# Delta rule's norms: sums of squares with the tokens as moving columns on column tiles, one root and reciprocal for four tiles, factors spread from row tiles

## The chip, the cores and the metric

One core of a Trainium2 chip runs the whole program in one launch. Its engines work side by side, each through its own instruction list in order: TensorE (PE, matmuls; PEld is its weight load), VectorE (DVE), ScalarE (ACT), GpSimd (POOL), and the queues that start DMAs (SP's above all). The metric is the device time of one execution in microseconds; the kernel before has a median of 2775.28 us over three runs (2774.92 to 2777.58).

## The reference, cut to what matters

The program is one block with a dilated attention and a gated delta rule, followed by two blocks of another kind, on 512 tokens of width 1024, in fp32. The change touches the norms of the first block's delta rule (8 heads of 64):

```python
def _l2norm(x):
    return x * lax.rsqrt(jnp.sum(x * x, axis=-1, keepdims=True) + EPS)

def _gated_deltanet(q, k, v, z, b_logit, a_logit, conv_w, a_log, dt_bias, norm_g):
    qkv = jax.nn.silu(_causal_conv(jnp.concatenate([q, k, v], axis=-1), conv_w))
    ...
    q = _l2norm(q.reshape(shp)) * HEAD_DIM ** -0.5
    k = _l2norm(k.reshape(shp))
    ...
    o = _chunk_gated_delta_rule(q, k, v, g, beta)
    o = _rmsnorm(o, norm_g) * jax.nn.silu(z.astype(jnp.float32).reshape(shp))
```

So each token has one factor per head for q, one for k, and later one for the output o.

## The kernel before

Activations lie feature by token: a tile is 128 partitions (features, two heads of 64) by 512 tokens, and the delta rule's q, k and v are four such tiles each (t = 0 to 3). A projection (`proj`, L133) is 24 matmuls of 512 columns into a PSUM tile of tag mm (3 buffers); its weights come by DMA, and ScalarE and VectorE split them into two fp32r parts (L103, L104). Everything else on PE writes PSUM tiles of tag mx (5 buffers).

`mixer1` (L581) writes its work in an order by hand: a list `d` of projections is worked off by `d.need` (up to a name) and `d.fill` (a number of microseconds' worth), and between them stand the steps of the delta rule. A scheduler then orders the instructions of every engine by priority, which follows the order written, and gives out the buffers; on the chip every engine goes through its list in that order, so a waiting instruction holds back what is behind it on its engine.

For tile t, L987 to L1000: `d.need("d{t}")` (three projections with convolution, `delta_in` L661), `delta_norm(t)` (L701), `delta_tok(t)` (L716: transposes of k and v), `delta_pairs(t)` (L732: products k by k and q by k, per head, times a decay), `q_decay(t)` (L759).

The norm itself: ScalarE squares q and k (L705). `head_rstd` (L680) sums each head's 64 features: a square's 128 x 128 piece is the stationary operand and two columns of ones (`bones`) move, so that the sums come out with tokens on partitions, 128 x 16 for q and k (L687). Root and reciprocal run on these (L467, L468). To bring the factors back to 512 columns, one column of them, repeated 64 times, is stationary and the identity moves (L696), 8 matmuls of 128 columns for q and as many for k. VectorE multiplies (L707).

At the end of `mixer1`, L1053 to L1060, `delta_out(t)` (L876) computes o for tile t (L886, L891), squares it (L894), multiplies by gain and gate (L897), and takes `head_rstd` for the one tile, then multiplies and splits into yd (L899, L900), which the last half of w_out's projection (`into_x`) reads.

Of the kernel before, what the change touches and what calls it, by code (L numbers as in the profile page):

```python
# [30 lines left out]
def cap(ap, off, dims):  # L31
    return bass.AP(ap.tensor, ap.offset + off, [list(ap.ap[0])] + [list(d) for d in dims])
# [37 lines left out]
class Net:  # L70
# [510 lines left out]
    def mixer1(self, extra, norm):  # L581
        nc, A, V = self.nc, self.A, self.V[0]
        v = nc.vector
# [93 lines left out]
                                       op0=ALU.mult, op1=ALU.add)  # L677
            nc.scalar.activation(out=dst, in_=dst, func=AF.Silu)

        def head_rstd(sqs):  # L680

            ps = self.mx()
            n = len(sqs)
            for j, sq in enumerate(sqs):
                for t in range(4):
                    c = 8 * j + 2 * t
# [5 lines left out]
            for j in range(n):  # L692
                ps = self.mx()
                for t in range(4):
                    for e in range(2):
                        nc.tensor.matmul(out=ps[64 * e:64 * e + 64, t * P:(t + 1) * P], lhsT=cap(c, 8 * j + 2 * t + e, [[0, 64]]),  # L696
                                         rhs=self.ident, start=True, stop=True)
                out.append(ps)
            return out

        def delta_norm(t):  # L701
            sqs = []
            for j in range(2):
                sqs.append(self.t2("dsq"))
                nc.scalar.activation(out=sqs[j], in_=qkv[j, t], func=AF.Square)  # L705
            for j, r in enumerate(head_rstd(sqs)):
                v.scalar_tensor_tensor(out=qkv[j, t], in0=qkv[j, t], scalar=0.125 if j == 0 else 1.0, in1=r,  # L707
                                       op0=ALU.mult, op1=ALU.mult)

        kdec = self.t8("kdec")  # L710
# [48 lines left out]
        def q_decay(t):  # L759
            eg = self.t2("eg")  # L760
            for e in range(2):
                nc.sync.dma_start(out=eg[64 * e:64 * e + 64],
                                  in_=bass.AP(es.tensor, es.offset + (2 * t + e) * T, [[0, 64], [1, T]]))
            v.tensor_tensor(out=q_all[:, t], in0=q_all[:, t], in1=eg, op=ALU.mult)
            nc.scalar.copy(out=st["egl"][:, t], in_=cap(eg, 63, [[64, 8]]))
# [107 lines left out]
            zs[t] = zs["all"][:, t]  # L873
            nc.scalar.activation(out=zs[t], in_=ps, func=AF.Silu)

        def delta_out(t):  # L876
            if t == 0:
                y[1] = [self.t8("yd", F32R) for _ in range(2)]
            ps = self.mx()
            S = st["S"]  # L880
            hs = [(2 * t + e, slice(64 * e, 64 * e + 64)) for e in range(2)]

            for tt in range(4):
                sl = slice(tt * P, tt * P + P)
                for h, o in hs:
                    nc.tensor.matmul(out=ps[o, sl], lhsT=rv[h // 4][:, tt, h % 4, 0:64], rhs=qkm[h // 4][:, h % 4, sl],  # L886
                                     start=tt == 0, stop=False)
            for c in range(1, 8):
                sl = slice(64 * c, 64 * c + 64)
                for h, o in hs:  # L890
                    nc.tensor.matmul(out=ps[o, sl], lhsT=S[o, c, 64 * t:64 * t + 64], rhs=q_all[o, t, sl],  # L891
                                     start=False, stop=c == 7)
            sq = self.t2("osq")
            nc.scalar.activation(out=sq, in_=ps, func=AF.Square, scale=0.125)  # L894
            yield
            o = self.t2("od")
            v.scalar_tensor_tensor(out=o, in0=ps, scalar=dng, in1=zs[t], op0=ALU.mult, op1=ALU.mult)  # L897
            r = head_rstd([sq])[0]
            v.tensor_tensor(out=o, in0=o, in1=r, op=ALU.mult)  # L899
            self.split(y[1][0][:, t], y[1][1][:, t], o)  # L900


        va = self.t8("va")
# [83 lines left out]
        for t in range(4):  # L987
            d.need(f"d{t}")
            if t == 0:
                d.need("ba")  # L990
            delta_norm(t)
            delta_tok(t)
            delta_pairs(t)
            q_decay(t)
            if t == 0:
                self.stash()
                self.load_rows()
            if t == 2:
                clear()
            d.fill(4, "va")  # L1000
        steps = solve()
        next(steps)
        self.setup2()
# [50 lines left out]
        next(outs[0])  # L1054
        for t in range(4):
            if t < 3:
                next(outs[t + 1])
            d.fill(C / 2)
            for _ in outs[t]:
                pass  # L1060
# [571 lines left out]
```

## Time and profile before

| | |
|---|---|
| profiled execution, device time | 2775.28 us |
| its span, first to last instruction | 2773.5 us |
| PE busy | 2708.2 us, 98% |
| VectorE busy | 1716.4 us, 62% |
| ScalarE busy | 1169.8 us, 42% |
| mean granted clock of PE, share of full speed | 0.991 |

Times are microseconds from the span's start. A matmul's length in a row is that of its way through the array, and the next one starts before it ends; what a matmul costs PE is the time to the next start. An fp32 matmul is two records (passes), an fp32r one is one. "[1.39 <-ACT dsq L705]" says how long the engine was idle before, and what ended it.

### The profile page before, as it was taken

What the parts mean: (1) busy time and instruction counts of PE and PEld (TensorE: products, weight loads), DVE (VectorE), ACT (ScalarE), POOL (GpSimd) and SP (SyncE); (2) the same over time, 40 slices, a digit from 0 to 9 for tenths busy, and PEclk for the clock granted to TensorE, in tenths of its full rate; (3) what the DMA queues carried; (4) which work ended last, traced back from release to release, by engine and by line L of the source; (5) the groups of instructions that cost most, each with busy time, mean ns of one, the idle gap of its engine ahead of it and who ended that gap; (6) DMA issues with size and microseconds to landing.
All of it is one profiled execution on the core that took longest, in us unless ns stands there. A gap on an engine that the chain in (4) does not pass through costs nothing. (4 is left out here: it accounts for less than half of the span.)

```text
span 2773.5 us, 42593 instructions
## 1 busy us (share of the span) xinstructions
PE 2708.2 (98%) x17518; PEld 2201.5 (79%) x17518; DVE 1716.4 (62%) x2690; ACT 1169.8 (42%) x1792; POOL 41.7 (2%) x79
## 2 busy tenths in 40 slices
PE   8999899999999999999999999999999999999998
PEld 4786678888887887887888888887877878888887
DVE  4687656747378777757466563568787575533334
ACT  5644333323255545444343232466454453422223
POOL 0011000000000000100000000000000000000000
PEclk9999999999999999999999999999999999999999
DMA  7464534646332222332446463322223334333332
GB/s 244 129 183 122 150 121 152 213 155 218 88 106 70 63 81 69 111 99 79 133 132 229 143 230 91 102 77 63 76 69 103 92 84 136 91 93 98 99 98 77
DMA packets 471315, 330.66 MB, mean 119 GB/s; under 512 B 15447, under 2 KB 426223, under 8 KB 469584
## 3 DMA queue, kind: packets, MB, share of 16 engines
q1 hardware_dynamic: 468176, 320.51, 38.1%
q0 software_dynamic: 2944, 7.43, 0.9%
q8 instruction: 138, 2.26, 0.3%
q14 instruction: 57, 0.47, 0.1%
HBM read 312.55 MB, written 13.24 MB: 117 GB/s over the span
## 5 line engine op out<-in xcount | busy, mean ns | idle before, releaser
L103 ACT CAST whi<-raw 128x1024 fp32r<-128x1024 f32 (+2 forms) x451 | 439.0, 975 | 1057.0 <-PE mm L124 748.7
L123 PE MATMUL mm<-hh,whi 128*128 128x512 f32 (+1 forms) x2248 | 865.4, 388 | 10.6 <-ACT hh L495 9.0
L124 PE MATMUL mm<-hl,whi 128*128 128x512 f32 (+1 forms) x2248 | 867.3, 386 | 1.6 <-DVE hl L496 1.2
L125 PE MATMUL mm<-hh,wlo 128*128 128x512 f32 (+1 forms) x2248 | 866.4, 386 | 0.0
L104 DVE TENSOR_TENSOR wlo<-raw,whi 128x1024 fp32r<-128x1024 f32 (+2 forms) x451 | 507.4, 1127 | 355.3 <-ACT whi L103 333.5
L123 PEld LDWEIGHTS mm<-hh,whi 128*128 128x128 f32 x2248 | 421.6, 189 | 102.7 <-ACT hh L495 12.9
L124 PEld LDWEIGHTS mm<-hl,whi 128*128 128x128 f32 x2248 | 424.4, 189 | 89.6 <-DVE hl L496 4.3
L125 PEld LDWEIGHTS mm<-hh,wlo 128*128 128x128 f32 x2248 | 424.2, 189 | 88.0 <-issue 4.6
L124 PE MATMUL mm<-hid,whi 128*128 128x512 f32 (+1 forms) x564 | 212.5, 377 | 0.0
L123 PE MATMUL mm<-hid,whi 128*128 128x512 f32 (+1 forms) x564 | 212.3, 376 | 0.0
L125 PE MATMUL mm<-hid,wlo 128*128 128x512 f32 (+1 forms) x564 | 211.9, 376 | 0.0
L500 DVE SCALAR_TENSOR_TENSOR x<-mm,mod,x 128x512 f32<-128x512 f32 (+1 forms) x116 | 80.4, 694 | 176.8 <-PE mm L125 176.0
L315 DVE SCALAR_TENSOR_TENSOR acc<-araw,cs,acc 128x512 f32<-128x512 f32 x224 | 167.9, 750 | 21.3 <-DMA araw<-in_w_ada_dram 16.5
L550 DVE TENSOR_TENSOR sg<-mm,sg 128x512 f32<-128x512 f32 x66 | 45.6, 691 | 149.6 <-PE mm L125 147.8
L1180 DVE TENSOR_TENSOR R<-R,tot 128x512 f32<-128x512 f32 x192 | 126.6, 685 | 10.1 <-PE mx L1145 7.1
L202 PE MATMUL mm<-wlo,hh 128*128 128x256 f32 x448 | 129.3, 289 | 0.8 <-DVE wlo L104 0.8
L203 PE MATMUL mm<-whi,hl 128*128 128x256 f32 x448 | 129.8, 290 | 0.0
L201 PE MATMUL mm<-whi,hh 128*128 128x256 f32 x448 | 129.0, 288 | 0.0
L123 PEld LDWEIGHTS mm<-hid,whi 128*128 128x128 f32 x564 | 106.1, 188 | 20.3 <-issue 1.2
L125 PEld LDWEIGHTS mm<-hid,wlo 128*128 128x128 f32 x564 | 106.1, 188 | 19.2
L124 PEld LDWEIGHTS mm<-hid,whi 128*128 128x128 f32 x564 | 106.1, 188 | 19.2
L202 PEld LDWEIGHTS mm<-wlo,hh 128*128 128x128 f32 x448 | 87.5, 195 | 1.7 <-DVE wlo L104 1.2
(376 smaller groups left out, 3359.2 us busy)
## 6 DMA issues: line engine op xcount, KB each, us to landing
raw<-in_w_in_dram SPq DMA_DIRECT2D x164, 512.0 KB
araw<-in_w_ada_dram SPq DMA_DIRECT2D x48, 1024.0 KB
raw<-in_w_ffn_in_dram SPq DMA_DIRECT2D x88, 512.0 KB
araw<-in_w_ada_dram SPq DMA_DIRECT2D x64, 256.0 KB
raw<-in_w_ffn_out_dram SPq DMA_DIRECT2D x32, 512.0 KB
raw<-in_w_gate_dram SPq DMA_DIRECT2D x22, 512.0 KB
raw<-in_w_up_dram SPq DMA_DIRECT2D x22, 512.0 KB
raw<-in_w_ada_dram SPq DMA_DIRECT2D x16, 512.0 KB
```

The costliest lines, as they stand in the source:

```text
L103: self.nc.scalar.copy(out=hi, in_=src)
L104: self.nc.vector.tensor_tensor(out=lo, in0=src, in1=hi.bitcast(F32), op=ALU.subtract)
L123: m(out=ps, lhsT=w[0], rhs=a[0], start=first, stop=False)
L124: m(out=ps, lhsT=w[0], rhs=a[1], start=False, stop=False)
L125: return m(out=ps, lhsT=w[1], rhs=a[0], start=False, stop=last)
L201: m(out=o, lhsT=a[0][:, sl], rhs=hi[:, k % 4], start=k == 0, stop=False)
L202: m(out=o, lhsT=a[0][:, sl], rhs=lo[:, k % 4], start=False, stop=False)
L203: m(out=o, lhsT=a[1][:, sl], rhs=hi[:, k % 4], start=False, stop=k == KT - 1)
L315: nc.vector.scalar_tensor_tensor(out=acc, in0=raw, scalar=cs[:, k:k + 1], in1=acc, op0=ALU.mult, op1=ALU.add)
L500: self.nc.vector.scalar_tensor_tensor(out=self.x(f)[:, sl], in0=ps[:, sl], scalar=g[:, f:f + 1], in1=self.x(f)[:, sl], op0=ALU.mult, op1=A ...
L550: nc.vector.tensor_tensor(out=sg, in0=pu, in1=sg, op=ALU.mult)
L1180: v.tensor_tensor(out=o, in0=o, in1=half(1 - c), op=ALU.mult)
```

## The change

Sums: the ones are now stationary (32 columns of `bones`: 16 for the one head, 16 for the other) and the square moves, 512 tokens at once, into one of the four 32-partition column tiles of a PSUM tile (`head_sums`, L686 of the new kernel). Four tiles' sums (q and k of two t) share one PSUM tile; one root and one reciprocal of 128 x 512 serve all (`head_factors`, L692, L693). Spread: a column that picks one row of a 32-row tile, repeated 64 times, is stationary and the 32 x 512 factors move (`head_spread`, L702), two matmuls for each of the four, from row tile 32c into column half 64e. `delta_norm` works on two t at once; `delta_out` is a generator over two t, with roots on 64 x 512.

```diff
-        def head_rstd(sqs):
-            ps = self.mx()
...
-                    nc.tensor.matmul(out=ps[:, c:c + 2], lhsT=sq[:, t * P:(t + 1) * P], rhs=cap(bones, 0, [[64, 2]]),
-                                     start=True, stop=True)
-            c = self.sp.tile([P, 16], F32, name="hc", tag="hc", bufs=2)
-            self.rsqrt(c[:, :8 * n], ps[:, :8 * n])
...
+        pick = consts[:, 448:450]
+        for e in range(2):
+            v.tensor_tensor(out=pick[:, e:e + 1], in0=i64[:, 16 * e:16 * e + 1], in1=i64[:, 32 + 16 * e:33 + 16 * e], op=ALU.add)
+
+        def head_sums(sq, ps, c):
+            nc.tensor.matmul(out=ps[32 * c:32 * c + 32], lhsT=bones[:, 48:80], rhs=sq, start=True, stop=True,
+                             tile_position=(0, 32 * c))
+
+        def head_factors(ps, n):
+            r = self.t2("hr")
+            nc.scalar.activation(out=r[:32 * n], in_=ps[:32 * n], func=AF.Sqrt, bias=self.eps[:32 * n])
+            v.reciprocal(out=r[:32 * n], in_=r[:32 * n])
+            return r
+
+        def head_spread(r, cs):
             out = []
+            for c in cs:
+                out.append(self.mx())
+                for e in range(2):
+                    nc.tensor.matmul(out=out[-1][64 * e:64 * e + 64], lhsT=cap(pick[32 * c:32 * c + 32], e, [[0, 64]]),
+                                     rhs=r[32 * c:32 * c + 32], start=True, stop=True, tile_position=(32 * c, 64 * e))
             return out
...
-        for t in range(4):
-            d.need(f"d{t}")
...
-            delta_norm(t)
-            delta_tok(t)
-            delta_pairs(t)
-            q_decay(t)
...
-            d.fill(4, "va")
+        for t in (0, 2):
+            ps = self.mx()
+            for u in (t, t + 1):
+                d.need(f"d{u}")
...
+                delta_sums(u, ps)
+            r = head_factors(ps, 4)
+            d.fill(C, "va")
+            delta_norm((t, t + 1), r)
+            for u in (t, t + 1):
+                delta_tok(u)
+                delta_pairs(u)
+                q_decay(u)
...
+                d.fill(4, "va")
...
-        outs = [delta_out(t) for t in range(4)]
...
+        a, b = [delta_out((2 * i, 2 * i + 1)) for i in range(2)]
+        next(a)
+        next(a)
+        d.fill(C / 2)
+        next(a)
+        next(b)
+        d.fill(C / 2)
+        next(b)
+        for _ in a:
+            pass
+        d.fill(C / 2)
+        next(b)
+        d.fill(C)
+        for _ in b:
+            pass
```

The order of the instructions moves with it. On PE before, from the first tile's spread (L696) to its pair products (L748); L123 to L125 are a projection's matmuls, L720 the transposes:

```order
L696 MATMUL mx<-c_ident,hc 64x128 x16
L125 MATMUL mm<-hh,wlo 128x512
L123 MATMUL mm<-hh,whi 128x512
L124 MATMUL mm<-hl,whi 128x512
...
L720 MATMUL mx<-c_ident,k_all 128x128 x4
L720 MATMUL mx<-c_ident,vd 128x128 x4
L748 MATMUL mx<-k_all 128x128 x8
L748 MATMUL mx<-q_all,k_all 128x128 x8
```

Six projection matmuls stand between, and 44 behind, before the next tile's sums. Now, from the spread of tiles 0 and 1 (L702) through both blocks (L728 are the transposes, L756 the products, with the buffers' numbers):

```order
L702 MATMUL mx_713<-hr_701,consts_367 64x512 x2
L728 MATMUL mx_720<-c_ident_83,k_all_387 128x128 x4
L728 MATMUL mx_727<-c_ident_83,vd_495 128x128 x4
L756 MATMUL mx_743<-k_all_387 128x128
L756 MATMUL mx_744<-k_all_387 128x128
...
L756 MATMUL mx_753<-q_all_386,k_all_387 128x128
L756 MATMUL mx_754<-q_all_386,k_all_387 128x128
...
L728 MATMUL mx_802<-c_ident_83,k_all_387 128x128 x4
L728 MATMUL mx_809<-c_ident_83,vd_687 128x128 x4
L123 MATMUL mm_905<-hh_264,whi_900 128x512
L756 MATMUL mx_825<-k_all_387 128x128 x3
```

Both tiles' blocks now follow each other with one projection matmul between them, and none between spread and transposes.

On DVE now, behind the pair's reciprocal (L693), where L715 are the multiplications by the factors, L736 and L738 read the transposes, L760 and L763 the products, and L746 and L747 make the decay (gb):

```order
L693 RECIPROCAL hr_701<-hr_701 128x512
L104 TENSOR_TENSOR wlo_984<-raw_982,whi_983 128x1024
L746 TENSOR_TENSOR gb_733<-gb_733,rt_385 128x512
L715 SCALAR_TENSOR_TENSOR q_all_386<-q_all_386,mx_704 128x512
L715 SCALAR_TENSOR_TENSOR k_all_387<-k_all_387,mx_707 128x512
L715 SCALAR_TENSOR_TENSOR q_all_386<-q_all_386,mx_710 128x512
L747 SCALAR_TENSOR_TENSOR gb_733<-gb_733,consts_367 128x512
L715 SCALAR_TENSOR_TENSOR k_all_387<-k_all_387,mx_713 128x512
L736 TENSOR_TENSOR kdec_390<-mx_720,rt_385 128x4x128
L738 TENSOR_TENSOR rr_391<-mx_720,rt_385 128x4x2x64
L746 TENSOR_TENSOR gb_738<-gb_738,rt_385 128x512
L760 TENSOR_TENSOR nt_763<-mx_743,gb_733 128x512
```

The four multiplications of two tiles stand together, ahead of the first tile's kdec, rr and nt, where before each tile had its own two ahead of its own block.

## Rows read from the trace of the kernel before

**Rows 1.** the page's busy times, whole span

```profile
PE 2708.2 (98%) x17518; PEld 2201.5 (79%) x17518; DVE 1716.4 (62%) x2690; ACT 1169.8 (42%) x1792; POOL 41.7 (2%) x79
```

**Rows 2.** table by stretch: length, busy per engine (instructions), clock, DMA, GB/s

```profile
80.00:172.00 92.00, 86.04 (x634) 73.89 (x633) 69.87 (x107) 57.34 (x82) 11.22 (x18) 0.94 0.49 150
...
373.00:402.00 29.00, 28.05 (x324) 23.26 (x324) 14.29 (x26) 10.03 (x18) 0.00 (x0) 1.00 0.09 26
```

**Rows 3.** instructions of L687 and L696: ns min/median/max, first and last start, form

```profile
L687 PE MATMUL mx<-consts,dsq x64: 165/251/353, 80.8 to 158.9; 128*128 128x2 f32 x64
...
L696 PE MATMUL mx<-c_ident,hc x192: 272/273/476, 85.9 to 395.3; 128*64 128x128 f32 x192
```

**Rows 4.** timeline, first tile's norm: start, length, engine, instruction, [idle before]

```profile
80.81 1.02 PE L687 MATMUL mx<-consts,dsq 128*128 128x2 f32 x8
...
81.69 0.47 PE L123 MATMUL mm<-hh,whi 128*128 128x512 f32 x1
...
85.94 1.97 PE L696 MATMUL mx<-c_ident,hc 128*64 128x128 f32 x32
...
87.84 0.19 PEld L125 LDWEIGHTS mm<-hh,wlo 128*128 128x128 f32 x1 [0.17 <-issue]
```

**Rows 5.** PE's timeline around L395, column tiles of 32

```profile
20.96 1.05 PE L395 MATMUL mx<-raw,cz 128*32 128x512 f32 x4
21.94 1.16 PE L483 MATMUL mx<-c_ident,col 128*128 128x128 f32 x8
...
31.95 1.07 PE L395 MATMUL mx<-raw,cz 128*32 128x512 f32 x8
```

**Rows 6.** timeline of the pair products, two row halves

```profile
90.31 1.16 PE L748 MATMUL mx<-k_all 64*128 64x128 f32 x16
...
91.30 1.34 PE L748 MATMUL mx<-q_all,k_all 64*128 64x128 f32 x16
```

**Rows 7.** instructions of L454, L453 and L468: ns min/median/max

```profile
L454 DVE RECIPROCAL rstd<-rstd x24: 3343/3353/3354, 882.3 to 2286.7; 128x512 f32<-128x512 f32 x24
...
L453 ACT ACTIVATE rstd<-mx,eps x24: 677/688/691, 881.6 to 2285.9; 128x512 f32<-128x512 f32 x24
...
L468 DVE RECIPROCAL hc<-hc x8: 194/228/253, 83.8 to 393.7; 128x16 f32<-128x16 f32 x4, 128x8 f32<-128x8 f32 x4
```

**Rows 8.** PE's waits, 30 to 175 us: total, times, longest

```profile
PE mx L687 <- ACT dsq L705: 3.7, 2, 2.3
...
PE mm L123 <- ACT q_all L673: 1.6, 1, 1.6
...
PE mx L646 <- DVE gt L643: 0.7, 1, 0.7
```

**Rows 9.** timeline of the projections' matmuls, at either clock

```profile
95.29 0.63 PE L124 MATMUL mm<-hl,whi 128*128 128x512 f32 x1
...
95.71 0.63 PE L125 MATMUL mm<-hh,wlo 128*128 128x512 f32 x1
...
98.88 0.39 PE L125 MATMUL mm<-hh,wlo 128*128 128x512 f32 x1
...
99.11 0.39 PE L123 MATMUL mm<-hh,whi 128*128 128x512 f32 x1
```

**Rows 10.** DVE's timeline behind the second tile's spread

```profile
111.80 0.69 DVE L707 SCALAR_TENSOR_TENSOR q_all<-q_all,mx 128x512 f32<-128x512 f32 x1 [2.68 <-PE mx L696]
112.40 0.68 DVE L738 TENSOR_TENSOR gb<-gb,rt 128x512 f32<-128x512 f32 x1
```

**Rows 11.** timeline of delta_out, first tile's norm

```profile
377.29 1.05 PE L687 MATMUL mx<-consts,osq 128*128 128x2 f32 x8
...
378.20 0.47 PE L125 MATMUL mm<-ya,wlo 128*128 128x512 f32 x1
...
381.02 1.09 PE L696 MATMUL mx<-c_ident,hc 128*64 128x128 f32 x16 [0.95 <-DVE hc L468]
...
381.95 1.04 PE L886 MATMUL mx<-qkm,rr 128*64 128x128 f32 x16
```

More of the change, by code (lines that the diff above doesn't have):

```diff
@@ L678, in delta_in @@
             nc.scalar.activation(out=dst, in_=dst, func=AF.Silu)
-        def head_rstd(sqs):
-            ps = self.mx()
-            n = len(sqs)
-            for j, sq in enumerate(sqs):
-                for t in range(4):
-                    c = 8 * j + 2 * t
-                    nc.tensor.matmul(out=ps[:, c:c + 2], lhsT=sq[:, t * P:(t + 1) * P], rhs=cap(bones, 0, [[64, 2]]),
-                                     start=True, stop=True)
-            c = self.sp.tile([P, 16], F32, name="hc", tag="hc", bufs=2)
-            self.rsqrt(c[:, :8 * n], ps[:, :8 * n])
-            out = []
[L692 to L698, printed above, removed]
-            return out
@@ L705, in delta_norm @@
-                nc.scalar.activation(out=sqs[j], in_=qkv[j, t], func=AF.Square)
-            for j, r in enumerate(head_rstd(sqs)):
-                v.scalar_tensor_tensor(out=qkv[j, t], in0=qkv[j, t], scalar=0.125 if j == 0 else 1.0, in1=r,
+                sq = self.t2("dsq")
+                nc.scalar.activation(out=sq, in_=qkv[j, t], func=AF.Square)
+                head_sums(sq, ps, 2 * (t % 2) + j)
+        def delta_norm(ts, r):
+            cs = [(j, t) for t in ts for j in range(2)]
+            for (j, t), p in zip(cs, head_spread(r, range(4))):
+                v.scalar_tensor_tensor(out=qkv[j, t], in0=qkv[j, t], scalar=0.125 if j == 0 else 1.0, in1=p,
@@ L874, in z_in, with delta_out @@
             nc.scalar.activation(out=zs[t], in_=ps, func=AF.Silu)
-        def delta_out(t):
-            if t == 0:
+        def delta_out(ts):
+            if y[1] is None:
                 y[1] = [self.t8("yd", F32R) for _ in range(2)]
-            ps = self.mx()
             S = st["S"]
[L881 to L894, printed above, removed]
-            yield
[L896 to L900, printed above, removed]
@@ new lines, in delta_out @@
+            sums, os = self.mx(), []
+            for i, t in enumerate(ts):
+                ps = self.mx()
+                hs = [(2 * t + e, slice(64 * e, 64 * e + 64)) for e in range(2)]
+                for tt in range(4):
+                    sl = slice(tt * P, tt * P + P)
+                    for h, o in hs:
+                        nc.tensor.matmul(out=ps[o, sl], lhsT=rv[h // 4][:, tt, h % 4, 0:64], rhs=qkm[h // 4][:, h % 4, sl],
+                                         start=tt == 0, stop=False)
+                for c in range(1, 8):
+                    sl = slice(64 * c, 64 * c + 64)
+                    for h, o in hs:
+                        nc.tensor.matmul(out=ps[o, sl], lhsT=S[o, c, 64 * t:64 * t + 64], rhs=q_all[o, t, sl],
+                                         start=False, stop=c == 7)
+                sq = self.t2("osq")
+                nc.scalar.activation(out=sq, in_=ps, func=AF.Square, scale=0.125)
+                os.append(self.t2("od"))
+                v.scalar_tensor_tensor(out=os[i], in0=ps, scalar=dng, in1=zs[t], op0=ALU.mult, op1=ALU.mult)
+                yield
+                head_sums(sq, sums, i)
@@ L903, in mixer1 @@
+            r = head_factors(sums, len(ts))
+            yield
+            for o, p, t in zip(os, head_spread(r, range(len(ts))), ts):
+                v.tensor_tensor(out=o, in0=o, in1=p, op=ALU.mult)
+                self.split(y[1][0][:, t], y[1][1][:, t], o)
         va = self.t8("va")
@@ L986, in mixer1 @@
         st["egl"] = self.cp.tile([P, 4, 8], F32, name="egl")
-        for t in range(4):
-            d.need(f"d{t}")
-            if t == 0:
-                d.need("ba")
-            delta_norm(t)
-            delta_tok(t)
-            delta_pairs(t)
-            q_decay(t)
[L995 to L999, printed above, removed]
-            d.fill(4, "va")
+        for t in (0, 2):
+            ps = self.mx()
+            for u in (t, t + 1):
+                d.need(f"d{u}")
+                if u == 0:
+                    d.need("ba")
+                delta_sums(u, ps)
[6 more added lines that the diff above has]
+                q_decay(u)
+                if u == 0:
+                    self.stash()
+                    self.load_rows()
+                if u == 2:
+                    clear()
+                d.fill(4, "va")
         steps = solve()
@@ L1052, in mixer1 @@
         extra.rest()
-        outs = [delta_out(t) for t in range(4)]
[L1054 to L1060, printed above, removed]
+        a, b = [delta_out((2 * i, 2 * i + 1)) for i in range(2)]
[13 more added lines that the diff above has]
+            pass
         d.rest()
```

4 lines of the change are left out of this document (1 added, 3 removed).

## Prediction

> **What bounds the kernel now.** I read the page's busy line first: the matmul engine (PE) is busy 2708.2 of 2773.5 us [rows 1]. It is the bound nearly everywhere, so an edit is worth what it takes off PE's stream, less what it adds in waits of PE. Then the table by stretch, for the two places that the change touches: 80 to 172 us (delta_norm, delta_tok, delta_pairs and q_decay of the four tiles, between the input projections) and 373 to 402 us (delta_out). In the first PE is busy 86.0 of 92.0 us and the vector engine (DVE) 69.9; in the second PE 28.05 of 29.0 and DVE 14.3 [rows 2]. So PE has little idle time to lose, and DVE has 22.1 and 14.7 us of room. Third, the groups of the lines that go, fourth the timeline around them and around the nearest relatives of what comes.
>
> The order of both kernels shows that from some ten microseconds behind delta_out the instructions are the same on every engine, so everything is decided in the first 415 us; the rest moves as one piece.
>
> **What goes from PE.** An fp32 matmul stands in the trace as two passes. The old sums (L687) are 64 passes in the norm stage and eight in each of delta_out's four calls, the old spread (L696) is 192 in all [rows 3]. Their price is from start to the next start, not the pipelined length: the first eight sum passes run from 80.81 to 81.69, 0.88 us; the 32 spread passes from 85.94 to 87.84, 1.90 us [rows 4]. A tile pair (q, k of one t) pays 2 x 0.88 + 1.90 = 3.7 us, four of them 14.6. In delta_out eight sum passes run from 377.29 to 378.20, 0.91 us, and 16 spread passes from 381.02 to 381.95, 0.93 us [rows 11]; four times 1.84 is 7.4. Together 22.0 us.
>
> **What comes to PE.** New sums: 12 matmuls with 512 moving columns on 32-column tiles. The nearest rows are L395's, 32 columns by 512, also on column tiles: four passes (two matmuls on two column tiles) take 20.96 to 21.94, 0.98 us; eight passes on four column tiles take 1.07 us in all [rows 5]. So a matmul costs about 0.95 us, and others on other column tiles lie beside it for nothing if they stand directly behind it. In the order they mostly don't: per two tiles the first q and k stand together, the second q and k alone, and delta_out's four each alone. That is 3 + 3 + 4 = 10 groups, 9.5 us. New spread: 8 matmuls (4 row tiles by 2 column halves) twice, 4 matmuls twice. The old trace has two row halves side by side: 16 passes of 128 columns take 90.31 to 91.30, 0.062 us a pass, as cheap as the old spread's 1.90 / 32 = 0.059 with its two column halves [rows 4, 6]. Four row tiles at once it does not show. Bounds: 0.95 us a group if all lie side by side, and 4 x 0.95 and 2 x 0.95 if only the two column halves do. I take 0.95, because both kinds of neighbours share the array in the rows: 4 x 0.95 = 3.8 us. So 13.3 us come, and PE's own work falls by 8.7 us (7.0 in the norm stage, where 6 + 2 groups cost 7.6; 1.7 in delta_out, where 4 + 2 cost 5.7). The upper bound of the spread takes 2 x 2.85 + 2 x 0.95 = 7.6 of it back.
>
> Behind the old column tiled group PE idles 0.17 us before the next full matmul [rows 4]; my 0.95 holds about half of such a step. "TensorEngine Tiling (Array Packing)" of the Trainium skill, Tiling Modes, Key Properties, says that a change of tiling mode (not of tile) empties the engine. That speaks against the change, which goes in and out of such modes 14 times where the old spread did 8 times; the rule names no price; with the row's 0.17 us for each of the six more it makes the sum below 1.0 us larger, 2777.5. I keep the sum without it, because half of such a step is in the 0.95 already, and leave the rest to the range.
>
> **What comes to DVE, and the waits of PE.** The old reciprocals are 128 x 16 and 128 x 8, 0.23 us; a reciprocal over 512 elements takes 3.35 us, the square root before it 0.69 [rows 7]. Four of the long ones cost DVE 4 x 3.35 - 8 x 0.23 = 11.6 us, half in each place. In the norm stage some 25 matmuls of other projections stand between the last sum and the spread (5.7 us at 0.23 each [rows 9]), which covers sum, root and reciprocal (0.3 + 0.7 + 3.4): nothing. What is late next is the block behind the spread. Before, six matmuls stood between a spread and the first transpose, and the block of transposes and pair products was one tile's. Now PE's queue holds two blocks in a row with one filler. PE's five side PSUM buffers (tag mx) come free only as DVE empties them, one operation per 0.60 us [rows 10]. Counted from the end of the spread, in DVE's new order: q done at 0.7, k at 1.3, second q 1.9, mask 2.5, second k 3.1, kdec 3.7, rr 4.3, then one each 0.6: nt 5.5, qkm 7.3, nt 7.9, qkm 8.5, kdec 9.7, rr 10.3. PE: transposes from 1.3 to 2.2; k products 2.2 to 3.2; q products need the buffer that rr frees, 4.3 to 5.3; second transposes to 6.2; second k products wait for nt, 7.9 to 8.9; second q products for rr, 10.3 to 11.3. PE's own work in it is 6.0 us, so it waits 5.3 us, twice: 10.6.
>
> Against that stand old waits: 3.7 (two), 1.6 and 0.7 us, 6.0 in all [rows 8]. They came because ScalarE reached the next tile's convolution and squares late; in the new order the second tile of a pair is through before the block, so its wait goes, and the one at the third tile's squares stays, which I price like the old ones of that kind at 2.5. Waits: 10.6 + 2.5 - 6.0 = +7.1 us. Behind old waits the granted clock falls to 1.2 GHz for a while: after the 1.6 us one, matmuls start 0.42 us apart instead of 0.23 [rows 9]; about eight of them, 1.5 us. Three such spells before, three after (two blocks, one wait): nothing, or 1.5 either way. Norm stage: -7.0 + 7.1 = about 0.
>
> delta_out: the chain for one pair is now square, sum, root, 3.35 us, spread, product, split. For the first two tiles the work of the third and fourth covers it. For the second pair, root to spread is 0.7 + 3.4 = 4.1 us, in which PE has the first spread's tail and three matmuls on the new yd tile; the first of those wait for ScalarE's yd. Walking it as above: about 1.4 us for yd, then 2.1 us for the second reciprocal, against 0.95 us at the old spread [rows 11]. With -1.7 of work that is +0.9; a spell of low clock behind the two waits, as likely as not, adds 0.8. Sum +1.7. Everything behind (w_out's strips) is ready by then.
>
> ScalarE loses four short roots and some table loads, and is not late anywhere in the new walk: no price. The two additions that build pick are two small DVE operations ahead of the stage: none.
>
> **Sum.** 0 + 1.7, made against the profiled execution (span 2773.5 us, 2775.28 us in all, which is also the median of the three runs): 2777; for the walk's DVE steps, which have no slack for ScalarE but also ignore that dense matmuls may slip in, I round toward no change: 2776.5.
>
> **Rivals.** (1) The blocks are not held: DVE has caught up before PE reaches the spread, and PE waits 1.5 us a block instead of 5.3. Then the norm stage is -7.0 + 3.0 + 2.5 - 6.0 = -7.5, and with +0.9 to -1 in delta_out the time is about 2768. For it: PE, not DVE, is the fuller engine [rows 2]; against it: the products that follow can't start before DVE's multiplications, wherever DVE stands. (2) Slower, one mechanism: DVE becomes the norm stage's bound. It must do 69.9 + 2 x 3.35 - 4 x 0.23 = 75.7 us there; if it keeps the 22.1 us of idle time that it has now (for DMAs, ScalarE and PE), the stage takes 97.8 instead of 92, +5.8, and with +1.7 behind 2783. It decides once its idle time can't shrink below 16.3 us. For it: several of its waits are for DMAs and ScalarE; against: one kind is the old spread's 2.7 us [rows 10], which the long reciprocal replaces. (3) The four row tiles do not lie side by side: +7.6 on PE, of which the blocks' waits hide none, 2784. (4) The sums or the spread of one matmul come out cheaper by lying beside their neighbours across the fillers: not in any row; at most 3 us, inside the forecast's own range.
>
> **Chances.** The forecast 0.53, its own range 2770 to 2781 (clock spells, six mode changes, a microsecond or two in either walk); rival 1 0.25; rival 2 0.13; rival 3 0.09. A measurement of this kernel tells 0.2% or 5.6 us from no change; so faster 0.25, same 0.53, slower 0.22. The range over all is 2767 to 2783.
>
> **What would show it.** Right: L686 groups about 0.95 us from start to next start, L702 groups of eight passes and sixteen passes equally long, reciprocals at 3.35, PE idle in the two blocks with DVE named as the releaser, some 5 us each, and two waits of PE around the last spread. Wrong: L702 over 3 us in the norm stage (rival 3); the blocks without waits (rival 1); DVE over 0.85 busy from the first reciprocal to the last qkm, and the transposes of the attention later by 6 us (rival 2). A moved time behind 415 us would break the argument as a whole.

## The result, and the profile after

The changed kernel takes 2790.7 us (median of four runs, 2787.15 to 2792.93); the kernel before, run beside it, takes 2775.1 (2772.15 to 2777.58). The ratio is 1.0055, with an interval of 1.0042 to 1.0068: some 15 us slower, outside the forecast range. The page of the profiled execution (span 2791.1 us, 2792.93 in all) answers to [rows 1]:

```profile
PE 2713.9 (97%) x17302; PEld 2190.1 (78%) x17302; DVE 1728.6 (62%) x2688; ACT 1160.3 (42%) x1781; POOL 41.7 (1%) x79
```

PE issues 216 matmul passes fewer, and is slower all the same. The table by stretch tells where. In each of the two fences the first row runs from the first sums of squares to the first matmul of the attention (a later end than in [rows 2], since the projections shift a little in the list), the second over delta_out to the first sums of the next norm; columns are length, busy time per engine (instructions), clock, DMA share and GB/s. Before:

```profile
80.81:194.74 113.93, 107.97 (x765) 92.70 (x764) 86.04 (x144) 66.90 (x95) 14.04 (x22) 0.96 0.55 164
373.32:414.64 41.32, 39.33 (x392) 33.31 (x391) 24.05 (x43) 16.36 (x29) 0.00 (x0) 1.00 0.22 65
```

After:

```profile
84.06:207.67 123.61, 105.21 (x630) 82.67 (x629) 91.20 (x140) 58.28 (x87) 13.95 (x22) 0.94 0.49 151
386.80:432.60 45.80, 40.72 (x318) 28.91 (x318) 29.91 (x41) 16.85 (x27) 0.00 (x0) 0.93 0.20 59
```

The norm stage is 9.7 us longer. PE is 2.8 us less busy there, but idle (length less busy) for 18.4 us instead of 6.0. Delta_out is 4.5 us longer, with the clock at 0.93 instead of 1.00. Together that is 14.2 of the 17.6 us between the two profiled spans (15.6 between the medians). The norm stage's window holds eight projection matmuls more than before (224 against 216 of L123 to L125), an estimated 1.8 us at 0.23 each, so not all of the 9.7 us is lost time. Behind delta_out nothing follows: from there to the last matmul both kernels need about 2352 us. Of the rest 3.3 us stand at the start (80.81 against 84.06), which the runs below deal with.

The new operations themselves are as cheap as priced. Per pass and per instruction, the groups of the new lines (ns min/median/max; [rows 3, 7] are their counterparts):

```profile
L686 PE MATMUL mx<-dsq,consts x16: 592/605/617, 84.1 to 153.6; 128*32 128x512 f32 x16
...
L702 PE MATMUL mx<-hr,consts x48: 587/637/1111, 103.9 to 409.2; 32*64 32x512 f32 x48
...
L693 DVE RECIPROCAL hr<-hr x4: 3341/3348/3353, 98.9 to 404.8; 128x512 f32<-128x512 f32 x2, 64x512 f32<-64x512 f32 x2
```

What is new are the waits of PE in the norm stage, where [rows 8] had 3.7, 1.6 and 0.7 us (total, times, longest):

```profile
PE mm L123 <- ACT q_all L673: 6.6, 1, 6.6
PE mm L201 <- ACT va L921: 4.2, 1, 4.2
PE mx L728 <- ACT gb L748: 2.0, 1, 2.0
PE mx L728 <- DVE k_all L715: 1.4, 1, 1.4
PE mx L268 <- DVE rr L738: 1.4, 1, 1.4
PE mx L756 <- DVE qkm L763: 1.0, 2, 0.5
PE mx L686 <- ACT dsq L709: 1.0, 1, 1.0
PE mx L756 <- DVE rr L738: 0.6, 1, 0.6
```

Those old waits were 6.0 us in all, and the rows above are 18.2. The two longest stand neither at a spread nor at a square. PE lacks one of the three buffers (tag mm) of its projections, because ScalarE has not copied the third tile's q, k and v out of them (L672, L673), and later the values' (L921). Following the first of them back through the engines shows why. ScalarE:

```profile
120.72 1.04 ACT L103 CAST whi<-raw 128x1024 fp32r<-128x1024 f32 x1 [4.43 <-PE mm L124]
124.39 0.63 ACT L748 ACTIVATE gb<-gb 128x512 f32<-128x512 f32 x1 [2.62 <-DVE gb L747]
125.76 0.63 ACT L748 ACTIVATE gb<-gb 128x512 f32<-128x512 f32 x1 [0.74 <-DVE gb L747]
126.30 0.57 ACT L672 COPY u<-mm 128x512 f32<-128x512 f32 x1
```

The copies stand behind the second tile's two exponentials of the decay (L748), and these wait for DVE:

```profile
121.80 1.23 DVE L104 TENSOR_TENSOR wlo<-raw,whi 128x1024 fp32r<-128x1024 f32 x1 [4.25 <-ACT whi L103]
122.94 0.68 DVE L746 TENSOR_TENSOR gb<-gb,rt 128x512 f32<-128x512 f32 x1
```

DVE has the decay's first operation (L746) behind a weight split (L104) that waits for ScalarE's half of it (L103), and that one waits until PE has used up an older strip, which is when PE runs out of buffers. So each engine of this chain is held by what stands ahead in its own list.

The decay's data are not what DVE waits for. Its row of L746 has no idle time in brackets, and in the trace the two transfers of the rows (gb) end at 116.88 and 118.91 us, 6.1 and 5.4 us before DVE reads them (122.94 and 124.27). In between DVE stands idle for 4.25 us, in front of the split. Still, the transfers' place on SP has moved against the blocks, and the runs below show that it matters:

```profile
103.76 0.58 SPq L246 DMA_DIRECT2D rows<-in_c_lm_dram  x1
...
113.09 1.99 SPq L745 DMA_DIRECT2D gb<-gs  x2
```

Between the blocks of the first and the second tile the program issues 21 small transfers (load_rows: one of L246, twenty of L241). Together with the first tile's eg (rows for q_decay, L770, 1.1 us) they hold SP for 9.3 us, and the second tile's decay rows (gb, L745) stand behind them. Before, the same transfers stood between the same two tiles (85.68 to 94.94 us), with the second tile's decay rows behind them:

```profile
98.22 3.62 SPq L737 DMA_DIRECT2D gb<-gs  x2
```

But there the two blocks were 25 us apart (their transposes start at 89.34 and 114.05 us), and DVE first used those rows at 112.40 [rows 10], 14 us after their issue. Now the second block starts 4 us behind the first (106.49 and 110.54).

"DMA: Bandwidth & Descriptors" of the Trainium skill, Issuing engines are not separate DMA queues, says that the sequencer's time to start a transfer is usually small beside the transfer. For each single transfer the trace agrees: a row transfer holds SP for about 0.3 us, while the two gb land 3.8 and 5.4 us after their issue. But in a row they hold SP for 9.3 us, longer than either gb takes to land.

The second wait is partly one for transfers. On SP the fourth tile's gb stand behind transfers of another stage's weights (L311) that wait for their buffers, and its eg comes later still:

```profile
153.01 13.97 SPq L311 DMA_DIRECT2D araw<-in_w_ada_dram  x3
...
170.26 0.78 SPq L745 DMA_DIRECT2D gb<-gs  x1
...
180.51 1.13 SPq L770 DMA_DIRECT2D eg<-es  x2
```

DVE waits 0.46 us for the second of these gb, which lands at 179.91. ScalarE has their exponential, one of setup2 that waits for DVE, and a small copy of eg ahead of the values' copies; the landing of eg is the last thing that it waits for:

```profile
181.86 0.63 ACT L748 ACTIVATE gb<-gb 128x512 f32<-128x512 f32 x1 [2.98 <-DVE gb L747]
184.59 0.21 ACT L280 ACTIVATE lbe<-lbe 128x8 f32<-128x8 f32 x1 [2.10 <-DVE lbe L279]
186.02 0.20 ACT L773 COPY egl<-eg 128x8 f32<-128x8 f32 x1 [1.22 <-DMA eg<-es]
186.13 1.55 ACT L921 COPY va<-mm 128x512 f32<-128x512 f32 x3
```

### The profile page after: what moved, and what is told of

Read it like the earlier page. It is cut to its first block, busy times and chain, and to the rows that moved or that the text cites. A ratio compares the mean times of both kernels' runs of the same rounds, so it can differ in the third digit from the quotient of the medians.

```text
span 2791.1 us, 42151 instructions
## 1 busy us (share of the span) xinstructions
PE 2713.9 (97%) x17302; PEld 2190.1 (78%) x17302; DVE 1728.6 (62%) x2688; ACT 1160.3 (42%) x1781; POOL 41.7 (1%) x79
## 4 chain that ended last, share of the span: by engine, by line
PE 60%; DVE 3%; ACT 2%; issue 1%; DMA 1%; POOL 0%; DVEq 0%; ACTq 0%; POOLq 0%
PE mm L124 16%; PE mm L123 16%; PE mm L125 16%; PE mx L124 2%; PE mx L123 2%; PE mx L125 2%; PE mx L1150 1%; PE mx L131 1%; PE mm L203 1%; PE mm L202 1%; PE mm L201 1%; ACT whi L103 1%; DMA rb<-ra 1%; PE mx L1171 0%; DVE R L1206 0%
## 5 line engine op out<-in xcount | busy, mean ns | idle before, releaser
L123 PE MATMUL mm<-hh,whi 128*128 128x512 f32 (+1 forms) x2248 | 863.7, 387 | 15.7 <-ACT hh L495 9.1
L103 ACT CAST whi<-raw 128x1024 fp32r<-128x1024 f32 (+2 forms) x451 | 439.1, 975 | 1047.5 <-PE mm L124 741.8
L125 PE MATMUL mm<-hh,wlo 128*128 128x512 f32 (+1 forms) x2248 | 866.0, 386 | 0.0
L104 DVE TENSOR_TENSOR wlo<-raw,whi 128x1024 fp32r<-128x1024 f32 (+2 forms) x451 | 507.3, 1126 | 364.5 <-ACT whi L103 340.5
L123 PEld LDWEIGHTS mm<-hh,whi 128*128 128x128 f32 x2248 | 420.6, 188 | 107.6 <-ACT hh L495 13.0
L125 PEld LDWEIGHTS mm<-hh,wlo 128*128 128x128 f32 x2248 | 423.9, 189 | 89.7 <-issue 6.3
L123 PE MATMUL mm<-hid,whi 128*128 128x512 f32 (+1 forms) x564 | 212.3, 376 | 0.0
L125 PE MATMUL mm<-hid,wlo 128*128 128x512 f32 (+1 forms) x564 | 211.9, 376 | 0.0
L123 PEld LDWEIGHTS mm<-hid,whi 128*128 128x128 f32 x564 | 106.1, 188 | 20.3 <-issue 1.2
L125 PEld LDWEIGHTS mm<-hid,wlo 128*128 128x128 f32 x564 | 106.1, 188 | 19.2
L201 PEld LDWEIGHTS mm<-whi,hh 128*128 128x128 f32 x448 | 87.9, 196 | 6.6 <-ACT va L921 5.1
```

Of the source, the lines that this page charges most:

```text
L103: self.nc.scalar.copy(out=hi, in_=src)
L104: self.nc.vector.tensor_tensor(out=lo, in0=src, in1=hi.bitcast(F32), op=ALU.subtract)
L123: m(out=ps, lhsT=w[0], rhs=a[0], start=first, stop=False)
L125: return m(out=ps, lhsT=w[1], rhs=a[0], start=False, stop=last)
L201: m(out=o, lhsT=a[0][:, sl], rhs=hi[:, k % 4], start=k == 0, stop=False)
```

## The experiments

Theories: A, the new arithmetic costs more than priced. Q, the order of two tiles' blocks in a row, with ScalarE's copies behind the second tile's decay. T, a form of Q: it is the place of SP's transfers that pairing breaks. D, DVE is simply behind. S, part of the loss lies in front of any changed instruction. Each kernel was run beside the kernel before and has one profile; "stage" is the length of the norm stage as above (113.9 before, 123.6 after), "out" that of delta_out (41.3 and 45.8).

| run | median us | ratio to before | stage | out |
|---|---|---|---|---|
| norm_only | 2785.39 | 1.0033 [1.0020, 1.0046] | 123.6 | 41.7 |
| out_only | 2782.18 | 1.0020 [1.0008, 1.0032] | 114.4 | 44.9 |
| pair_old | 2787.45 | 1.0038 [1.0027, 1.0050] | 127.0 | 41.2 |
| each_new | 2780.59 | 1.0017 [1.0004, 1.0029] | 117.8 | 41.5 |
| decay_first | 2783.32 | 1.0025 [1.0015, 1.0035] | 120.0 | 44.9 |
| decay_va | 2785.38 | 1.0036 [1.0024, 1.0048] | 119.4 | 44.9 |
| rows_later | 2783.2 | 1.0030 [1.0015, 1.0046] | 114.4 | 44.6 |
| out_norecip | 2771.1 | 0.9986 [0.9976, 0.9996] | 114.5 | 40.5 |
| norm_rows | 2776.9 | 1.0004 [0.9993, 1.0015] | 114.6 | 40.9 |
| norm_decay_rows_va | 2776.82 | 1.0000 [0.9990, 1.0010] | 114.2 | 41.2 |
| each_rows_va | 2780.93 | 1.0015 [1.0006, 1.0024] | 117.6 | 41.2 |
| before_rows | 2778.92 | 1.0004 [0.9994, 1.0015] | 113.6 | 40.6 |

**norm_only and out_only: the two halves of the change.**

Norm_only is the changed kernel with delta_out(t) of before, and head_rstd for it. Out_only is the kernel before with delta_out(ts) of the changed kernel, and pick, head_sums, head_factors and head_spread for it.

> The new sums, root, reciprocal and spread in the norm stage alone (two tiles at a time), delta_out as before. Theory Q (queues): the loss sits mainly in the norm stage, where ScalarE's list puts the second tile's exponentials of the decay ahead of the copies that empty the projections' PSUM buffers, so that PE stands for some 7 us behind the first pair and 4 to 5 us behind the second; then 2783 to 2787 us, with both waits in the profile. Theory A (arithmetic): the new matmuls and the long reciprocal themselves cost more than priced, in equal parts in both places; then about 2782 us, with waits at the spread. Theory S (start): 4.65 us of the loss stood in the profile before any changed instruction and belong to this program's start; then the start is late here too (first matmul of the projections' second strip group, L577, at about 53.7 us).

> The new arithmetic in delta_out alone, in twos, norm stage as before. Theory Q: the offset between the two profiles grew by 3.6 us across delta_out, so 2778 to 2780 us. Theory A: half of the loss, 2782 us. Theory S: the start is as before (L577 at 49 us).

The halves add up: 0.33% and 0.20% against 0.55% for both. Norm_only has both long waits (6.6 and 3.7 us), as Q expected. S is not borne out: L577 comes at 49.4 us in norm_only, not at 53.7, and out_only, whose norm stage is the old one, has its first projection matmul as late as the changed kernel (38.2 us against 38.3; 35.1 before, 35.5 in norm_only). Decay_first below, which has the whole change, starts at 37.0 and has L577 at 48.9. So the late start does not go with the changed instructions; with one profile for each kernel it stays open whether it belongs to the execution or to the program.

**pair_old: two tiles at a time, old arithmetic.**

```diff
-            delta_norm(t)
...
+            cs = []
...
+                cs.append(delta_sums(u))
+            d.fill(C, "va")
+            for u, c in zip((t, t + 1), cs):
+                delta_norm(u, c)
```

Delta_sums holds the old squares, sums and short reciprocal of a tile, delta_norm its old spread and the multiplications.

> Two tiles at a time in the norm stage with the old arithmetic (sums by 16 small matmuls, short reciprocals, spread by 16 matmuls a tile); the matmuls stand in PE's list as in the changed kernel. Delta_out as before. Theory Q: the waits of 7 and 4 to 5 us are there although no sum, reciprocal or spread has changed; 2783 to 2790 us. Theory A: without the new arithmetic nothing is lost; 2773 to 2778 us.

This run decides between A and Q. Nothing of the new arithmetic is in it, and the loss is there in full (1.0038), with waits of 5.7 and 3.7 us at the same two places. DVE and ScalarE read as in the changed kernel, with the decay behind a weight split and the copies behind the decay:

```profile
122.31 1.22 DVE L104 TENSOR_TENSOR wlo<-raw,whi 128x1024 fp32r<-128x1024 f32 x1 [2.88 <-ACT whi L103]
123.45 0.68 DVE L748 TENSOR_TENSOR gb<-gb,rt 128x512 f32<-128x512 f32 x1
```

```profile
121.23 1.04 ACT L103 CAST whi<-raw 128x1024 fp32r<-128x1024 f32 x1 [4.39 <-PE mm L124]
...
125.42 0.63 ACT L750 ACTIVATE gb<-gb 128x512 f32<-128x512 f32 x1 [2.61 <-issue]
125.95 0.57 ACT L672 COPY u<-mm 128x512 f32<-128x512 f32 x1
```

Here too the rows of this L748 lay ready, landed at 117.44 us; in norm_only they landed at 113.48 and 114.04 and were read at 118.64 and 119.97.

The run also prices the arithmetic, since PE's other matmuls in the stage are those of norm_only. Pair_old and norm_only in the table by stretch:

```profile
80.76:207.78 127.02, 113.77 (x774) 97.65 (x773) 85.62 (x140) 62.49 (x92) 13.98 (x22) 0.93 0.47 147
```

```profile
79.79:203.43 123.64, 107.11 (x629) 85.20 (x629) 91.28 (x140) 58.39 (x87) 13.95 (x22) 0.92 0.49 151
```

At nearly the same clock PE is 6.7 us less busy with the new sums and spread; the forecast's term was 7.0.

**each_new: new arithmetic, one tile at a time.**

```diff
         def delta_norm(t):
...
+                head_sums(sq, ps, j)
+            r = head_factors(ps, 2)
+            for j, p in enumerate(head_spread(r, range(2))):
```

> The new arithmetic in the norm stage, but one tile at a time in the order of before (a 64x512 reciprocal per tile, four in all; sums of q and k on two column tiles, spread from two row tiles). Delta_out as before. Theory Q: without the two tiles' blocks in a row there is no long wait; PE's work falls by some 6 us and the chain through the reciprocal (4.4 us) is covered by the 17 to 46 projection matmuls that stand between sums and spread; 2766 to 2775 us. Theory A: the long reciprocal and the mode changes cost as in the changed kernel, four times instead of two: 2783 us or more.

Both missed: slower than before, but by half of what A expected. The wait behind the first pair is gone. Two others are there. One is 2.7 us at the first tile's transposes, behind DVE's multiplication of k. The long reciprocal is not what makes it: with 17 projection matmuls between these sums and their spread, PE waits 0.25 us for it at the spread (88.49). Behind the reciprocal DVE has a weight split that waits for ScalarE, and only then q and k:

```profile
89.17 1.23 DVE L104 TENSOR_TENSOR wlo<-raw,whi 128x1024 fp32r<-128x1024 f32 x1 [0.74 <-ACT whi L103]
90.32 0.68 DVE L735 SCALAR_TENSOR_TENSOR q_all<-q_all,mx 128x512 f32<-128x512 f32 x1
```

The other is 4.3 us for the values' copies: ScalarE's list again, with setup2's constants in front of them.

**decay_first, decay_va, rows_later: three edits of the order, with the change as it is.**

```diff
+                if u == t:
+                    delta_decay(t)
+                    delta_decay(t + 1)
                 delta_tok(u)
...
-        self.setup2()
         d.extra = extra
         d.need("va")
+        self.setup2()
...
-                if u == 0:
+                if u == 1:
                     self.stash()
                     self.load_rows()
```

The first piece is decay_first (delta_decay is gb's transfer, L746, L747 and the exponential, taken out of delta_pairs); decay_va has the first and the second; rows_later has the third alone.

> The changed kernel with the decay tiles of both tiles of a pair (their transfers, DVE's two operations and ScalarE's exponentials, gb) put ahead of the first tile's transposes, so that in ScalarE's list the second tile's exponentials stand in front of the weight splits and the copies, not behind the splits. Theory Q: PE's wait of 6.8 us behind the first pair (before L123 on the third tile's projections) falls to under 2 us, the one before the values' projection stays at 4 to 5, since the list of the later constants (setup2) still stands ahead of the values' copies; 2783 to 2786 us. Rival D (DVE is simply behind: two long reciprocals and two tiles' work in a row): the wait moves to another place with the same length; 2789 to 2792 us.

> As the run with the decay tiles first, and the second layer's constants (setup2: two transposes, their copies, an exponential that waits for DVE) issued behind the values' projection instead of ahead of it. Theory Q: both long waits are gone, 2778 to 2782 us; the rest of the loss is delta_out's. Rival D: 2788 to 2792 us.

> The changed kernel with the 22 small row transfers (stash and load_rows) issued behind the second tile of the first pair instead of between its tiles, so that the second tile's decay rows do not queue behind them on SP. Rival T (the transfers are what is late): the 6.8 us wait falls by the 4 us or so by which the transfers come earlier; 2785 to 2787 us. Theory Q: the exponentials' rows were in the buffer before DVE reached them (DVE stood at a weight split that waited for ScalarE), so the wait stays within 1.5 us of 6.8; 2789 to 2792 us.

Decay_first took away 8 us (1.0025 against 1.0055), of which its norm stage shows 3.6 (123.6 to 120.0), and its time is the one expected by Q, but its waits are not. The wait for the copies shrank to 2.0 us, and a new one of 5.5 appeared at the third tile's squares. Here ScalarE does wait for a transfer:

```profile
112.44 1.53 SPq L246 DMA_DIRECT2D rows<-in_c_lm_dram  x1
...
121.27 1.09 SPq L773 DMA_DIRECT2D eg<-es  x2
```

```profile
124.67 0.20 ACT L776 COPY egl<-eg 128x8 f32<-128x8 f32 x1 [3.35 <-DMA eg<-es]
```

The row transfers now hold up the second tile's other rows (eg). ScalarE waits for those with a small copy, and the third tile's activations and squares stand behind it. So Q's cure moved the wait, and the row transfers still stand ahead of what the second tile needs. Decay_va has a 3.6 us wait at the squares and 1.5 at the values; its median is no better than decay_first's, which Q did not expect.

In rows_later 22 transfers (21 by the trace, a miscount) only change places, and the stage falls to 114.4 us, which is nearly all of the loss there. Q's expectation for it, no gain, was wrong; T's was exceeded. SP issues the second tile's gb 5.8 us earlier, DVE reaches the decay before the weight splits (116.28 and 121.74), and ScalarE before its half of the second:

```profile
107.26 4.45 SPq L745 DMA_DIRECT2D gb<-gs  x2
```

```profile
115.68 0.68 DVE L746 TENSOR_TENSOR gb<-gb,rt 128x512 f32<-128x512 f32 x1
...
121.74 1.22 DVE L104 TENSOR_TENSOR wlo<-raw,whi 128x1024 fp32r<-128x1024 f32 x1
```

```profile
118.13 0.63 ACT L748 ACTIVATE gb<-gb 128x512 f32<-128x512 f32 x1 [2.16 <-DVE gb L747]
...
120.38 1.04 ACT L103 CAST whi<-raw 128x1024 fp32r<-128x1024 f32 x1 [0.24 <-PE mm L124]
121.33 0.58 ACT L672 COPY u<-mm 128x512 f32<-128x512 f32 x1
```

The copies come 5.0 us earlier than in the changed kernel. The 6.6 us wait is 2.0, and the one for the values 2.3. Two things changed with this edit: the transfers land earlier (110.28 and 115.08 us, not 116.88 and 118.91), and the decay has another place in DVE's and ScalarE's lists, although only transfers were moved in the program. No run separates them, but the traces say which weighs more. In the changed kernel the rows lay ready for over 5 us, so Q was right about them, and an earlier landing by itself would have moved nothing there. In the new order the old landing would have held DVE up for some 1.2 us (116.88 against 115.68; an estimate), of the 5.0 gained. The rest goes to the order of the lists. Why these change with the transfers' place is not shown. The whole run's ratio (1.0030) is wide and would leave 0.2% for delta_out and 0.1% for chance; the next run is the cleaner one.

**norm_rows, norm_decay_rows_va, each_rows_va, before_rows: the cure with the old delta_out, and a control.** Norm_rows is norm_only with the edit of rows_later; the second has all three edits; each_rows_va is each_new with the last two; before_rows is the kernel before with the row transfers moved.

> The new norm stage alone (delta_out as before), with the 22 row transfers behind the second tile of the first pair. Theory T (after the last runs: the order of SP's transfers is what pairing breaks): the norm stage takes as long as before (114 us from the first sums to the first attention matmul, where the run of the norm stage alone took 123.6), so 2775 to 2778 us, no different from before. If the loss of the norm stage is the arithmetic, it stays at 2783 to 2786.

> As the run before it, with the decay tiles of both tiles of a pair ahead of the first tile's transposes and the second layer's constants behind the values' projection. Theory T: no transfer for the second tile queues behind others, PE has no wait over 3 us in the norm stage, and PE's smaller work (some 4 us less) comes through: 2769 to 2774 us. If the walk through DVE is the limit after all, waits of 2 to 5 us remain elsewhere: 2776 to 2782.

> The new arithmetic one tile at a time, with the row transfers behind the second tile and the constants behind the values' projection; delta_out as before. The 4.7 us wait before the values' projection goes, the 3.3 us wait at the first spread (reciprocal on the path) stays: 2774 to 2778 us.

> Control: the kernel before with nothing but the row transfers moved behind the second tile. There the second tile's decay comes some 20 us behind the first's, so the transfers hold up nothing: 2773 to 2778 us, no difference. If they are a cost by themselves wherever they stand, it gains some microseconds: 2768 to 2772.

Norm_rows is T's case: from 1.0033 to 1.0004, no different from before, by an edit that moves transfers alone (and by it the lists, as in rows_later). The control shows that this is no gain of the move as such (1.0004 on the kernel before, stage 113.6). Norm_rows by stretch:

```profile
79.62:194.20 114.58, 104.11 (x630) 81.12 (x629) 90.58 (x140) 58.40 (x87) 13.95 (x22) 0.97 0.52 163
```

Against norm_only PE is idle 6.0 us less (16.5 to 10.5; its longest waits are now 2.4 us for the values and 2.0 for the copies) and busy 3.0 us less at the same instructions, with the clock at 0.97 instead of 0.92. A long wait is paid twice: once as idle time, and once as matmuls at the lower of the two clock levels behind it. In the changed kernel the matmuls behind the 6.6 us wait start some 0.43 us apart up to 130.66, and 0.23 from 131.03 on.

Norm_decay_rows_va has no wait over 2.0 us and is still no faster than before: the miss of the most hopeful expectation. Waits of 1 to 2 us at seven places stand where one of 6.6 stood, 10 us idle in all as in norm_rows. Each_rows_va keeps its wait at the values (4.7 us) although setup2 was moved in the program: in ScalarE's list its constants (L269 to L280) still stand ahead of the values' copies, which begin at 178.83, and so does a small copy that waits for the fourth tile's eg:

```profile
178.72 0.20 ACT L793 COPY egl<-eg 128x8 f32<-128x8 f32 x1 [1.55 <-DMA eg<-es]
```

Neither kernel beats the one before.

**out_norecip: the price of the long reciprocals in delta_out.**

```diff
             nc.scalar.activation(out=r[:32 * n], in_=ps[:32 * n], func=AF.Sqrt, bias=self.eps[:32 * n])
-            v.reciprocal(out=r[:32 * n], in_=r[:32 * n])
```

> The new arithmetic in delta_out alone (as the run of that), without its two reciprocals: the outputs are multiplied by the root instead of its inverse. If the 3.35 us reciprocal is what PE waits for at the second spread, the last wait of 2.2 us goes and the time falls by 2 to 3 us against the run with reciprocals, to 2779 to 2780; the waits for ScalarE's squares (1.1 and 1.0) and for the split tile (1.4) stay. If the waits are other than this, it stays at 2782 us.

Out_only and out_norecip over delta_out:

```profile
375.37:420.22 44.85, 39.76 (x318) 28.48 (x318) 29.92 (x41) 16.83 (x27) 0.00 (x0) 0.96 0.21 60
```

```profile
372.57:413.08 40.51, 38.17 (x319) 27.36 (x318) 23.49 (x39) 16.86 (x27) 0.00 (x0) 1.00 0.23 67
```

The stage is 4.3 us shorter, more than the 2 to 3 expected: the wait at the last spread falls from 2.0 to 0.8 (now for the root), the 0.8 at the first one goes, the wait for the split tile, which follows the first reciprocal, falls from 1.3 to 0.4, and the clock stays at full speed. The medians differ by more, 0.34%, with intervals wide enough for half of that. Without its reciprocals the new delta_out is 0.8 us shorter than the old; with them it is 3.5 longer.

## Why the prediction was wrong

The step that failed is in the part on the waits of PE: "ScalarE ... is not late anywhere in the new walk: no price". The walk took the two blocks' own operations through PE, DVE and the side buffers. It left out what else stands in the lists: on DVE and ScalarE the weight splits of the projections, which in the changed kernel stand ahead of the second tile's decay, on ScalarE the projections' copies behind that decay, and SP's transfers altogether. Measured in its place: PE waits 6.6 us for ScalarE's copies of the third tile and 4.2 us for those of the values, 10.8 of 18.2 us of listed waits, where the forecast had nothing for either; and slow matmuls follow. Pair_old shows that the order alone loses everything. Norm_rows shows that the row transfers' place in the program decides whether it does; the traces show that the long wait itself is one for the lists, with the data lying ready. How the transfers' place comes to change the lists stays open.

Point by point:

- **PE's own work** was right in the main. A group of sums alone takes 0.98 us from start to start (389.91 to 390.89; forecast 0.95). Sixteen spread passes on four row tiles last 1.11 us, eight on two row tiles 1.09, so four row tiles do lie side by side and rival 3 falls. The two groups in which q and k stand together do not wholly lie side by side, since k's square is ready some 0.5 us behind q's: they take 1.37 and 1.50 us to the next start, 1 us more in all than forecast. Net 6.7 us less in the norm stage by pair_old and norm_only, for 7.0. The forecast's 0.17 us of idle time stands in a row of the weight load (PEld), not of PE. The step that it looked for is elsewhere, and smaller: the projection matmul ahead of a group takes 0.32 us to the next start (389.59 below), where ahead of the old sums, which use the whole array, it takes 0.23 (80.58 to 80.81 before). The rule that a change of tiling mode empties the engine ("TensorEngine Tiling (Array Packing)" of the Trainium skill, Tiling Modes, Key Properties) agrees with such a step.

```profile
103.94 1.11 PE L702 MATMUL mx<-hr,consts 32*64 32x512 f32 x16
...
389.59 0.40 PE L125 MATMUL mm<-ya,wlo 128*128 128x512 f32 x1
389.91 1.05 PE L686 MATMUL mx<-osq,consts 128*32 128x512 f32 x2
```

- **The reciprocal**: 3.35 us, and covered in the norm stage as said (no wait of PE at either spread). In each_new, with 17 matmuls of cover instead of 25, PE waits 0.25 us for it.
- **The blocks behind the spread** were over-priced: 10.6 us forecast, 5.0 in the four listed waits that belong to them (2.0, 1.4, 1.0, 0.6). In both blocks PE went on with some products while DVE multiplied. The third tile's squares cost 1.0 instead of 2.5. Without the failed step the norm stage comes out about even, as forecast and as norm_rows shows: 114.6 against 113.9, with the eight projection matmuls more in it. Both sides of that balance are smaller than forecast (PE 4.5 us more idle and 3.9 less busy, for 7.1 and 7.0), so the near zero was in part luck.
- **Rival 2** (DVE as the bound) gave the right sign and is not the cause: DVE is busy 91.2 of 123.6 us and stands idle for 4.25 us within the chain that ends in PE's longest wait. Even its time, 2783, and with it the whole stated range lies under the measured one.
- **delta_out** was forecast at +1.7 and came out at +3.5 in out_only, +4.5 in the changed kernel. Its two named waits are right to 0.1 us (for the split tile 1.4, for the second reciprocal 2.1; 1.3 and 2.0 measured in both kernels). Two were not there in the walk, which had the first pair's chain and the third tile's square covered by the other tiles' products: 1.0 us for the square and 0.8 for the first reciprocal. These make the difference to out_only. The spell at the lower clock, taken as even odds, came (0.96, and 0.93 in the changed kernel). The rows of the changed kernel for three of the waits:

```profile
398.13 1.05 PE L686 MATMUL mx<-osq,consts 128*32 128x512 f32 x2 [0.97 <-ACT osq L904]
...
401.95 1.09 PE L702 MATMUL mx<-hr,consts 32*64 32x512 f32 x8 [0.79 <-DVE hr L693]
...
408.25 1.98 PE L702 MATMUL mx<-hr,consts 32*64 32x512 f32 x8 [1.99 <-DVE hr L693]
```

That everything is decided in the first 415 us held.

## What to carry to other kernels

When steps are drawn together, walk every list that they share with all that stands in it, other work's splits and copies and SP's transfers too, not the moved steps alone. A wait shows up far from where it arises, here as PE waiting for ScalarE's copies, so follow a new wait back engine by engine until it ends at a transfer or at the waiting engine itself. Where it passes a transfer, ask when the data landed and when they were read: here they lay ready for over 5 us, and the order of the lists was the wait. And test order and arithmetic apart: the old arithmetic in the new order showed in one run that the loss does not need the new matmuls.

## What the runs showed of the hardware

Eight fp32 matmuls of 512 columns on four row and two column tiles (16 passes, 1.11 us) take hardly longer than four on two row tiles (8 passes, 1.09 us). A reciprocal costs the same on 64 partitions as on 128, 3.34 and 3.35 us for 512 elements.

Stretches without any changed instruction differ between executions: the first projection matmul came between 35.1 and 38.3 us, the stretch from the first matmul of the attention to delta_out took 176 to 183 us, and the 14,850 matmul records behind delta_out took 2349 to 2353 us, at granted clocks of 1.00 (2349.3 us in out_norecip) and 0.99 (2352.8 us in out_only).

So one profile's span can differ from another's by several microseconds without any change there; the length of the stage that was changed repeats within 0.6 us (113.9, 114.4, 114.5 for the old norm stage).
